# Loading the first modulation weights in 16 pieces, and x and ctx from ScalarE's queue, in a one-core transformer trunk

## The chip, the cores and the metric

The kernel runs on one core of one Trainium2 chip. The metric is the device time of one execution in microseconds (us). Three runs are shown, and one more execution was profiled.

## What is computed

The reference is a trunk of two layers over 256 latent tokens `x` and 256 context tokens `ctx`, each 1024 wide, in float32. The part in front of the first matrix product is this:

```
mod   = silu(c) @ w_mod[l] + b_mod[l]            # 6 x 1024: sh1, sc1, g1, sh2, sc2, g2
mod_c = silu(c_ctx) @ w_mod[l] + b_mod[l]
h  = rmsnorm(x,   norm_mix[l]) * (1 + sc1)  + sh1
hc = rmsnorm(xc,  norm_mix[l]) * (1 + sc1c) + sh1c
z  = h @ w_in[l];  zc = hc @ w_in[l]             # D_IN = 8160 columns, split in 13 parts
...
```

After it come three token mixers (gated linear attention, windowed attention, latent attention), their merge, and a gated feed-forward; layer 1 drops the context stream's output. The first third of `w_mod[0]` (columns 0 to 2047: `sh1`, then `sc1`) and all of `x` and `ctx` are needed before any column of `z` can be computed.

## The kernel before

Everything is kept transposed: 8 tiles of 128 features by 512 tokens (256 of `x`, 256 of `ctx`). A float32 product is made of three float32r products: each operand is split in a high part (a rounding copy on ScalarE) and a low part (a subtraction on VectorE), and TensorE adds high times high (L248), high times low (L249) and low times high (L250). Weights arrive in staging buffers `ws` (three, of 128 x 2048) by loads on SyncE's queue, and are split in blocks of 128 x 1024 into `wh` (ScalarE, L171) and `wl` (VectorE, L172), four buffers each. The tile scheduler puts the instructions of each engine in an order when the program is built; an engine then runs them in that order.

The start of the program (`program`, L1357 to L1375) goes like this:

- `start` (L273) issues the loads of `c`, `c_ctx` and a part of the constants, then the eight quarter-megabyte loads `tok` of `x` and `ctx` (L286), all on SyncE's queue, and `first_units` (L399) issues the first third of `w_mod` in eight loads of 1 MB: three go into the three `ws` buffers, four into the two large buffers that later hold `h` (`hh` and `hl`, here named `wshh` and `wshl`), and the eighth into a `ws` buffer again, once that one has been read. GpSimd's queue loads the biases and gains (`rows`, L296) and the rest of the constants.
- `turn_x` (L356) transposes the tokens on TensorE (L364), copies them out (`x`, L367 and L369) and sums their squares (`acc`, L519 to L523).
- `mod_half(1)` (L416) makes the scales `sc1`: four steps (a `tick` each) of four matmuls over one 1 MB load (L427), then a copy (`modsb`, L432), four transposes (`modt`, L435) and, on VectorE, the sums into `modT` (L440, L441) and the gains (L454). `mod_half(0)` does the same for the shifts `sh1`. `vectors` (L331) transposes `rows`.
- `rstd` (L525) makes the reciprocal root on TensorE (`st`, L531), VectorE (`var`) and GpSimd (`rs`, L537), and `spread` (L540) makes of it a 128 x 512 tile `R` (L556).
- `scaled` (L561) makes `xr` = x times gain times R in 16 instructions on VectorE (L568), and `shifted` (L572) makes of them the high part of h, `hh`, in 16 instructions on ScalarE (L581) and the low part, `hl`, in 16 on VectorE (L582).

The first products are in `gla` (L967): `need` (L183) calls for three blocks of `w_in` (`krgk`, the first query block and the first key block), and `gemms` (L252) makes 144 matmuls of them, 48 each, into the three accumulators `mm`. From them `gkT` (L961, L962), `q` and `k` (L814) are copied out, the gate matmuls `gk` follow (L758, L759), then four groups of value matmuls (L795 to L797, 24 each, `mm` again) and then the first gate product of 512 columns (L248). The `krgk` block comes in three loads of short rows (L155 to L157) behind a GpSimd memset (L152), the others by L137.

Of the kernel before, what the change touches and what calls it, by code (L numbers as in the profile page):

```python
# [7 lines left out]
F32 = mybir.dt.float32  # L8
# [9 lines left out]
P = 128  # L18
D = 1024
KT = 8  # L20
T = 512
# [32 lines left out]
class Trunk:  # L54
# [218 lines left out]
    def start(self):  # L273

        nc, A = self.nc, self.A
# [6 lines left out]
        tok = [[self.tl([P, T], F32, "yh" if b < 2 else "yl", "tok") for _ in range(2)] for b in range(4)]  # L282
        for f in range(2):
            for b in range(4):
                src = A["x" if b < 2 else "ctx"][0, b % 2 * P:(b % 2 + 1) * P, f * T:(f + 1) * T]
                nc.sync.dma_start(out=tok[b][f], in_=src)  # L286
        self.first_units()
        self.prefetch()

# [109 lines left out]
    def first_units(self):  # L399


        nc = self.nc
        ws = lambda: self.tl([P, self.STAGE], F32, "ws", "ws")
        room = [ws() for _ in range(3)]
        for tag in ("hh", "hl"):
            both = self.tl([P, KT * T + 32], F32, tag, "ws" + tag)
            room += [both[:, i * self.STAGE:(i + 1) * self.STAGE] for i in range(2)]
        self.first = {}
        for half in (1, 0):
            for pair in range(4):  # L410
                st = room.pop(0) if room else ws()
                src = self.A["w_mod"][0, pair * 256:(pair + 1) * 256, half * D:(half + 1) * D]
                nc.sync.dma_start(out=st.rearrange("p (k c) -> p k c", k=2), in_=src.rearrange("(k p) c -> p k c", p=P))
                self.first[half, pair] = st

    def mod_half(self, half):  # L416


        nc = self.nc
        ps = self.ps("mod")  # L420
        for pair in range(4):
            w = self.first[half, pair]
            for i in range(2):
                for q in range(2):
                    j = 2 * i + q
                    c0 = i * D + q * 512
                    self.in_order(nc.tensor.matmul(ps[32 * j:32 * j + 32, :], lhsT=self.cs[:, 2 * pair + i, :],  # L427
                                                   rhs=w[:, c0:c0 + 512], start=pair == 0, stop=pair == 3))
            if pair < 3:
                yield  # L430
        sb = self.t([P, 512], name="modsb")
        nc.scalar.activation(out=sb, in_=ps, func=AF.Copy)  # L432
        pt = self.ps("modt")
        for s in range(4):
            self.in_order(nc.tensor.transpose(pt[:, s * P:(s + 1) * P], sb[:, s * P:(s + 1) * P], self.ident))  # L435
        pv = pt.rearrange("p (s i q w) -> p i q s w", s=4, i=2, q=2)
        b0 = half * 8
        m = self.modT[0][:, b0:b0 + 8, :].rearrange("p (q s) w -> p q s w", q=2)
        v = self.vec[0][:, b0:b0 + 8].rearrange("p (q s o) -> p q s o", q=2, o=1).to_broadcast([P, 2, 4, 2])
        nc.vector.tensor_tensor(out=m, in0=pv[:, 0, :, :, 0:2], in1=v, op=ALU.add)  # L440
        nc.vector.tensor_tensor(out=m, in0=pv[:, 1, :, :, 0:2], in1=m, op=ALU.add)  # L441
        if half:
            self.mod_gain(0, 0)
        yield
# [912 lines left out]
    def program(self):  # L1357
        nc = self.nc
        self.bg = None
        tok, rows = self.start()  # L1360
        acc = self.turn_x(tok)
        self.background(self.mod_half(1))
        self.tick(3)
        self.vectors(rows)
        rs = self.rstd(acc, D)
        self.tick(1)
        R = self.spread(rs)
        self.background(self.mod_half(0))
        self.tick(1)
# [2 lines left out]
        for l in range(2):  # L1372
# [35 lines left out]
            q = self.swa_q(l, 0, nq, h)  # L1408
# [111 lines left out]
```

## Time and profile before

| | us |
|---|---|
| median of three runs (lowest, highest) | 1897.33 (1896.89, 1897.68) |
| the profiled execution | 1899.36 |
| its span, first to last instruction | 1897.6 |
| TensorE busy in the span | 1859.0 |
| ScalarE busy in the span | 888.7 |
| VectorE busy in the span | 1231.8 |

The span is what the profile's clock counts from its first instruction; 1.8 us of the profiled execution lie outside it. All times of the trace are us from the start of the span. A row of a timeline has its start, its length, engine, line, operation, tile written and tiles read, shape, count, and in brackets the time for which the engine had been idle and what ended that. "SPq" and "POOLq" are queues that issue loads.

### The profile page before, as it was taken

What the parts mean: (1) busy time and instruction counts of PE and PEld (TensorE: products, weight loads), DVE (VectorE), ACT (ScalarE), POOL (GpSimd) and SP (SyncE); (2) the same over time, 40 slices, a digit from 0 to 9 for tenths busy, and PEclk for the clock granted to TensorE, in tenths of its full rate; (3) what the DMA queues carried; (4) which work ended last, traced back from release to release, by engine and by line L of the source; (5) the groups of instructions that cost most, each with busy time, mean ns of one, the idle gap of its engine ahead of it and who ended that gap; (6) DMA issues with size and microseconds to landing.
All of it is one profiled execution on the core that took longest, in us unless ns stands there. A gap on an engine that the chain in (4) does not pass through costs nothing.

```text
span 1897.6 us, 28869 instructions
## 1 busy us (share of the span) xinstructions
PE 1859.0 (98%) x11482; PEld 1594.6 (84%) x11482; DVE 1231.8 (65%) x2514; ACT 888.7 (47%) x1617; POOL 29.6 (2%) x47
## 2 busy tenths in 40 slices
PE   6999999999999999989999999999999999999998
PEld 4888887788877777888888888899998888899997
DVE  6756454565376655578776755768666678777775
ACT  4654333455454554342223233556455566655554
POOL 2000000000000000000000000000000000000000
PEclk8999999999999999999999999999999999999999
DMA  8533124413134312425555542342443324356553
GB/s 289 145 100 90 56 89 156 137 47 103 53 112 155 99 58 78 138 77 177 178 185 184 182 168 78 106 137 81 123 136 92 112 91 128 99 195 198 172 171 104
DMA packets 217870, 241.01 MB, mean 127 GB/s; under 512 B 18110, under 2 KB 204740, under 8 KB 212616
## 3 DMA queue, kind: packets, MB, share of 16 engines
q1 hardware_dynamic: 216888, 238.13, 39.5%
q8 instruction: 90, 1.47, 0.3%
q0 software_dynamic: 560, 0.52, 0.1%
q10 hardware_dynamic: 288, 0.52, 0.1%
q14 instruction: 44, 0.36, 0.1%
HBM read 234.96 MB, written 4.19 MB: 126 GB/s over the span
## 4 chain that ended last, share of the span: by engine, by line
PE 90%; DVE 4%; ACT 2%; issue 2%; DMA 1%; POOL 1%; SPq 0%; DVEq 0%; POOLq 0%; ACTq 0%
PE mm L248 23%; PE mm L249 23%; PE mm L250 23%; PE S L1138 2%; PE pt L728 2%; PE po L1237 2%; PE po L934 2%; PE po L1151 2%; PE mm L797 2%; PE mm L795 2%; PE mm L796 2%; DVE wl L172 1%; PE S L1218 1%; PE S L1219 1%; ACT wh L171 1%
## 5 line engine op out<-in xcount | busy, mean ns | idle before, releaser
L171 ACT ACTIVATE wh<-ws 128x1024 fp32r<-128x1024 f32 (+3 forms) x352 | 361.9, 1032 | 595.8 <-PE mm L249 449.3
L172 DVE TENSOR_TENSOR wl<-ws,wh 128x1024 fp32r<-128x1024 f32 (+3 forms) x352 | 416.9, 1188 | 296.8 <-ACT wh L171 258.0
L248 PE MATMUL mm<-hh,wh 128*128 128x512 f32 (+1 forms) x1312 | 462.9, 354 | 8.3 <-ACT hh L607 4.5
L249 PE MATMUL mm<-hl,wh 128*128 128x512 f32 (+1 forms) x1312 | 460.2, 351 | 1.0 <-DVE hl L582 0.9
L250 PE MATMUL mm<-hh,wl 128*128 128x512 f32 (+1 forms) x1312 | 460.1, 351 | 0.0
L248 PEld LDWEIGHTS mm<-hh,wh 128*128 128x128 f32 x1312 | 247.5, 189 | 45.5 <-ACT hh L607 5.4
L249 PEld LDWEIGHTS mm<-hl,wh 128*128 128x128 f32 x1312 | 247.8, 189 | 35.0 <-DVE hl L582 1.1
L250 PEld LDWEIGHTS mm<-hh,wl 128*128 128x128 f32 x1312 | 248.2, 189 | 31.9
L248 PE MATMUL mm<-yh,wh 128*128 128x512 f32 (+1 forms) x384 | 130.9, 341 | 0.0
L250 PE MATMUL mm<-yh,wl 128*128 128x512 f32 (+1 forms) x384 | 129.3, 337 | 0.0
L249 PE MATMUL mm<-yl,wh 128*128 128x512 f32 (+1 forms) x384 | 129.2, 336 | 0.0
L249 PE MATMUL mm<-sl,wh 128*128 128x256 f32 (+1 forms) x373 | 122.1, 327 | 0.0
L250 PE MATMUL mm<-sh,wl 128*128 128x256 f32 (+1 forms) x373 | 122.0, 327 | 0.0
L248 PE MATMUL mm<-sh,wh 128*128 128x256 f32 (+1 forms) x373 | 120.7, 325 | 0.0
L709 ACT ACTIVATE p<-S,stat 128x512 f32<-128x512 f32 (+1 forms) x144 | 87.2, 614 | 30.5 <-DVE stat L700 22.8
L248 PE MATMUL mm<-xh,wh 128*128 128x258 f32 x352 | 100.2, 285 | 0.1
L250 PE MATMUL mm<-xh,wl 128*128 128x258 f32 x352 | 99.9, 284 | 0.0
L249 PE MATMUL mm<-xl,wh 128*128 128x258 f32 x352 | 99.9, 284 | 0.0
L698 DVE TENSOR_REDUCE stat<-S 128x1 f32<-128x512 f32 (+1 forms) x144 | 81.5, 595 | 22.0 <-PE S L1138 14.0
L473 DVE SCALAR_TENSOR_TENSOR macc<-ws,cs,macc 128x512 f32<-128x512 f32 x112 | 77.9, 745 | 19.1 <-DMA ws<-in_w_mod 19.0
L248 PEld LDWEIGHTS mm<-yh,wh 128*128 128x128 f32 x384 | 72.6, 189 | 13.1 <-issue 3.3
L1267 DVE SCALAR_TENSOR_TENSOR x<-mm,modT,x 128x256 f32<-128x256 f32 x96 | 44.0, 481 | 60.5 <-PE mm L250 60.3
(311 smaller groups left out, 3463.2 us busy)
## 6 DMA issues: line engine op xcount, KB each, us to landing
ws<-in_w_in SPq DMA_DIRECT2D x54, 1024.0 KB, 5.9
ws<-in_w_mod SPq DMA_DIRECT2D x44, 1024.0 KB, 6.0
ws<-in_w_ffn_in SPq DMA_DIRECT2D x40, 1024.0 KB, 5.1
ws<-in_w_ffn_out SPq DMA_DIRECT2D x16, 896.0 KB, 4.8
ws<-in_w_in SPq DMA_DIRECT2D x18, 512.0 KB, 4.5
ws<-in_w_pa SPq DMA_DIRECT2D x8, 1024.0 KB, 5.2
ws<-in_w_pc SPq DMA_DIRECT2D x8, 1024.0 KB, 6.2
ws<-in_w_pb SPq DMA_DIRECT2D x8, 1024.0 KB, 5.2
```

The source lines that it names most:

```text
L171: self.nc.scalar.activation(out=hv, in_=src, func=AF.Copy)
L172: self.nc.vector.tensor_tensor(out=lv, in0=src, in1=hv.bitcast(F32), op=ALU.subtract)
L248: mm(ps, lhsT=a, rhs=rh[:, n0:n1], start=first and k == 0, stop=False)
L249: mm(ps, lhsT=a, rhs=rl[:, n0:n1], start=False, stop=False)
L250: mm(ps, lhsT=b, rhs=rh[:, n0:n1], start=False, stop=last and k == kt - 1)
L473: nc.vector.scalar_tensor_tensor(out=a, in0=b, scalar=c, in1=a, op0=ALU.mult, op1=ALU.add)
L698: nc.vector.reduce_max(out=mx[:, i:i + 1], in_=s, axis=AX.X)
L709: nc.scalar.activation(out=p, in_=s, func=AF.Exp, scale=scale, bias=nb[:, i:i + 1], accum_out=sm[:, i:i + 1])
L728: nc.tensor.transpose(ps[:, j * 256 + b * P:j * 256 + (b + 1) * P], p[b][:, c:c + P], self.ident)
L795: nc.tensor.matmul(ps[:, :256], lhsT=a, rhs=hi[:, kk, :], start=k8 == 0, stop=False)
L796: nc.tensor.matmul(ps[:, :256], lhsT=a, rhs=lo[:, kk, :], start=False, stop=False)
L1267: self.nc.vector.scalar_tensor_tensor(out=self.X[j][:, c], in0=ps[:, c], scalar=self.modT[l][:, b0 + j, w:w + 1], in1=self.X[j][:, c], op0 ...
```

## The change

It does four things. The eight loads of `x` and `ctx` are issued by ScalarE. The first third of `w_mod` comes in 16 loads of half a megabyte (128 rows of 1024 columns, 4 KB a row) in place of eight of 1 MB with two such row blocks each; eight go into the four `wh` and four `wl` buffers (named `wwh` and `wwl` there), and eight into the two buffers of `h` (`whh`, `whl`), so that the three `ws` buffers are free for `w_in` from the start. `mod_half` reads the pieces. And the ticks are moved: `rstd` follows two steps of `mod_half(1)` in place of three, and `vectors` comes after it.

```diff
@@ start @@
-                nc.sync.dma_start(out=tok[b][f], in_=src)
+                nc.scalar.dma_start(out=tok[b][f], in_=src)
@@ first_units @@
-        ws = lambda: self.tl([P, self.STAGE], F32, "ws", "ws")
-        room = [ws() for _ in range(3)]
+        room = [self.tl([P, D], F32, tag, "w" + tag) for tag in ("wh", "wl") * 4]
         for tag in ("hh", "hl"):
-            both = self.tl([P, KT * T + 32], F32, tag, "ws" + tag)
-            room += [both[:, i * self.STAGE:(i + 1) * self.STAGE] for i in range(2)]
-        self.first = {}
-        for half in (1, 0):
-            for pair in range(4):
-                st = room.pop(0) if room else ws()
-                src = self.A["w_mod"][0, pair * 256:(pair + 1) * 256, half * D:(half + 1) * D]
-                nc.sync.dma_start(out=st.rearrange("p (k c) -> p k c", k=2), in_=src.rearrange("(k p) c -> p k c", p=P))
-                self.first[half, pair] = st
+            four = self.tl([P, KT * T + 32], F32, tag, "w" + tag)
+            room += [four[:, i * D:(i + 1) * D] for i in range(4)]
+        self.first = room
+        for i, st in enumerate(room):
+            k, c0 = i % 8, (1 - i // 8) * D
+            nc.sync.dma_start(out=st, in_=self.A["w_mod"][0, k * P:(k + 1) * P, c0:c0 + D])
@@ mod_half @@
-            w = self.first[half, pair]
             for i in range(2):
+                w = self.first[(1 - half) * 8 + 2 * pair + i]
                 for q in range(2):
                     j = 2 * i + q
-                    c0 = i * D + q * 512
                     self.in_order(nc.tensor.matmul(ps[32 * j:32 * j + 32, :], lhsT=self.cs[:, 2 * pair + i, :],
-                                                   rhs=w[:, c0:c0 + 512], start=pair == 0, stop=pair == 3))
+                                                   rhs=w[:, q * 512:(q + 1) * 512], start=pair == 0, stop=pair == 3))
@@ program @@
-        self.tick(3)
-        self.vectors(rows)
+        self.tick(2)
+        rs = self.rstd(acc, D)
+        self.vectors(rows)
-        rs = self.rstd(acc, D)
-        self.tick(1)
+        self.tick(2)
```

The scheduler makes another order of this, on three places. A row below is an instruction (line, operation, tile written and tiles read, elements of a partition row written), in brackets the completion counters that it waits for: an engine's, or one of eight for loads (DMAHW); xN is a count of equal rows. Lines after the change are lower by 5.

On ScalarE, between the second `modsb` copy and the split of the gate weights `wgkh`, before:

```order
L432 ACTIVATE modsb<-mod 128x512 [waits PE_49]
L171 ACTIVATE wh<-ws 128x1024 [waits DMAHW4_49,DMAHW5_49,DMAHW3_49,Pool_49]
L581 ACTIVATE hh<-xr,modT_68 128x256 [waits DMAHW7_49,DMAHW6_49,DVE_49]
L581 ACTIVATE hh<-xr,modT_68 128x256 x15
L171 ACTIVATE wh<-ws 128x1024 [waits DMAHW6_49]
L265 ACTIVATE wgkh<-wgk 128x512 [waits DMAHW3_49,DMAHW2_49,DMAHW4_49,DMAHW1_49,DMAHW5_49,DMAHW0_49,Pool_49]
```

and with the change:

```order
L427 ACTIVATE modsb<-mod 128x512 [waits PE_49]
L576 ACTIVATE hh<-xr,modT_68 128x256 [waits DMAHW5_49,DMAHW4_49,DMAHW6_49,DMAHW3_49,DVE_49]
L576 ACTIVATE hh<-xr,modT_68 128x256 x15
L171 ACTIVATE wh<-ws 128x1024 [waits DMAHW4_49,DMAHW5_49,DMAHW3_49,Pool_49]
L171 ACTIVATE wh<-ws 128x1024 [waits DMAHW6_49]
L171 ACTIVATE wh<-ws 128x1024 [waits DMAHW7_49]
L265 ACTIVATE wgkh<-wgk 128x512 [waits DMAHW3_49,DMAHW2_49,DMAHW4_49,DMAHW1_49,DMAHW5_49,DMAHW0_49,Pool_49]
```

The first split of `w_in` (the `krgk` block) stood ahead of the 16 `hh` instructions and now stands behind them; VectorE's order moves in the same way, its first `wl` from ahead of the 16 `hl` to behind them.

On TensorE, the first products (`mm_427` is the krgk block's accumulator before; `mm_439`, `mm_440` and `mm_441` are those of krgk, query and key with the change, each with its own `wh` and `wl`), before:

```order
L248 MATMUL mm_427<-hh_345,wh_399 128x256 [waits Activation_49]
L249 MATMUL mm_427<-hl_346,wh_399 128x256 [waits DVE_49]
L250 MATMUL mm_427<-hh_345,wl_400 128x256
L248 MATMUL mm_427<-hh_345,wh_399 128x256 [waits Activation_49]
L249 MATMUL mm_427<-hl_346,wh_399 128x256 [waits DVE_49]
L250 MATMUL mm_427<-hh_345,wl_400 128x256
```

and with the change, behind the first four (high times high and high times low of krgk and of the query block), the next twelve:

```order
L250 MATMUL mm_439<-hh_357,wl_412 128x256 [waits DVE_49]
L248 MATMUL mm_439<-hh_357,wh_411 128x256
L249 MATMUL mm_439<-hl_358,wh_411 128x256
L248 MATMUL mm_441<-hh_357,wh_419 128x256 [waits Activation_49]
L249 MATMUL mm_441<-hl_358,wh_419 128x256
L250 MATMUL mm_440<-hh_357,wl_416 128x256 [waits DVE_49]
L250 MATMUL mm_439<-hh_357,wl_412 128x256
L248 MATMUL mm_440<-hh_357,wh_415 128x256
L249 MATMUL mm_440<-hl_358,wh_415 128x256
L250 MATMUL mm_440<-hh_357,wl_416 128x256
L248 MATMUL mm_439<-hh_357,wh_411 128x256
L250 MATMUL mm_441<-hh_357,wl_420 128x256 [waits DVE_49]
```

Before, the 48 matmuls of krgk come first, each group of three behind the `hh` and `hl` that it reads; now the three blocks take turns, and the 15 matmuls ahead of the last row shown wait for one split after the other; that row waits for the third `wl`, and the 129 from it on for nothing more.

On ScalarE further on, with the change, between the splits for the value products (`wh_425`, `wh_429`) and the copies out of the three accumulators:

```order
L171 ACTIVATE wh_425<-ws_423 128x1024 [waits DMAHW6_49]
L171 ACTIVATE wh_429<-ws_423 128x1024 [waits DVE_49,PE_49]
L956 ACTIVATE gkT_586<-mm_439 16x512 [waits PE_49,Pool_49]
L809 ACTIVATE q_599<-mm_440 128x512 [waits PE_49]
L809 ACTIVATE k_601<-mm_441 128x512 [waits PE_49]
```

`wh_429` takes the buffer of `wh_411`, so its wait on TensorE is for the last matmul of krgk that reads it; the same split stood before ahead of the krgk copies with no wait on TensorE, since krgk was done early. The first value matmul waits for the copy `q_599`, whose accumulator it takes. Past the value products each engine's instructions stand in the same order as before.

## Rows read from the trace of the kernel before

**Rows 1.** The page's part 1: busy us, share of the span, instructions.

```profile
PE 1859.0 (98%) x11482; PEld 1594.6 (84%) x11482; DVE 1231.8 (65%) x2514; ACT 888.7 (47%) x1617; POOL 29.6 (2%) x47
```

**Rows 2.** Windows of 50 us: window, length, busy us of PE, PEld, DVE, ACT, POOL, clock, DMA.

```profile
0.00:50.00 50.00, 34.04 (x195) 22.30 (x196) 31.04 (x77) 22.95 (x44) 11.75 (x26) 0.83 0.85 283
50.00:100.00 50.00, 50.00 (x361) 44.34 (x360) 34.41 (x72) 28.35 (x47) 0.00 (x0) 1.00 0.44 129
...
300.00:350.00 50.00, 50.00 (x243) 34.60 (x242) 20.12 (x37) 11.38 (x21) 1.01 (x1) 1.00 0.55 188
```

**Rows 3.** Timeline, start: ScalarE's first instruction, and loads issued on SyncE's queue.

```profile
0.74 1.28 ACT L322 ACT_TABLE_LOAD   x1 [0.74 <-PEq L1510]
...
1.94 0.90 SPq L286 DMA_DIRECT2D tok<-in_x  x2
...
6.33 3.46 SPq L413 DMA_DIRECT2D ws<-in_w_mod  x3
...
16.82 1.34 SPq L413 DMA_DIRECT2D ws<-in_w_mod  x1
```

**Rows 4.** Windows, columns as in rows 2; the last two are DMA share and GB/s.

```profile
4.00:9.00 5.00, 2.22 (x9) 1.75 (x9) 0.53 (x3) 0.22 (x1) 3.08 (x7) 1.00 0.95 306
...
18.00:31.00 13.00, 10.04 (x44) 4.15 (x48) 5.31 (x17) 1.88 (x5) 2.45 (x4) 0.56 1.02 420
```

**Rows 5.** Timeline of TensorE, 14 to 40 us.

```profile
21.22 1.93 PE L427 MATMUL mod<-ws,cs 128*32 128x512 f32 x8 [1.42 <-DMA ws<-in_w_mod]
23.08 0.69 PE L337 MATMUL ps<-cst,rows 128*128 128x128 f32 x2
23.56 1.71 PE L531 MATMUL st<-ones,acc 128*128 128x1 f32 x8
25.20 1.93 PE L427 MATMUL mod<-wshh,cs 128*32 128x512 f32 x8
...
34.38 1.03 PE L427 MATMUL mod<-ws,cs 128*32 128x512 f32 x8
...
37.99 0.39 PE L248 MATMUL mm<-hh,wh 128*128 128x256 f32 x1 [1.19 <-ACT hh L581]
39.31 0.39 PE L249 MATMUL mm<-hl,wh 128*128 128x256 f32 x1 [0.94 <-DVE hl L582]
```

**Rows 6.** Timeline of VectorE, 10 to 60 us.

```profile
16.17 3.07 DVE L523 TENSOR_TENSOR acc<-acc,sq 128x512 f32<-128x512 f32 x4
...
30.42 6.35 DVE L568 SCALAR_TENSOR_TENSOR xr<-x,gain,R 128x256 f32<-128x256 f32 x16 [0.76 <-PE R L556]
...
37.04 0.17 DVE L441 TENSOR_TENSOR modT<-modt,modT 128x16 f32<-128x16 f32 x1
37.63 1.23 DVE L172 TENSOR_TENSOR wl<-ws,wh 128x1024 fp32r<-128x1024 f32 x1 [0.42 <-ACT wh L171]
...
49.25 2.36 DVE L172 TENSOR_TENSOR wl<-ws,wh 128x1024 fp32r<-128x1024 f32 x2
```

**Rows 7.** Timeline of ScalarE, 36 to 60 us.

```profile
36.48 1.06 ACT L171 ACTIVATE wh<-ws 128x1024 fp32r<-128x1024 f32 x1 [0.39 <-DMA ws<-in_w_in]
...
37.44 6.48 ACT L581 ACTIVATE hh<-xr,modT 128x256 fp32r<-128x256 f32 x16
...
47.06 0.59 ACT L961 ACTIVATE gkT<-mm 16x512 fp32r<-16x512 f32 x1 [0.72 <-PE mm L250]
...
58.73 0.60 ACT L814 ACTIVATE q<-mm 128x512 f32<-128x512 f32 x1
```

**Rows 8.** Windows, columns as in rows 2: TensorE's clock in the first products.

```profile
40.10:43.50 3.40, 3.40 (x18) 3.40 (x18) 3.40 (x9) 3.40 (x10) 0.00 (x0) 0.50 0.96 280
43.50:58.00 14.50, 14.50 (x125) 14.37 (x124) 10.27 (x20) 6.64 (x11) 0.00 (x0) 1.00 0.64 187
```

**Rows 9.** Timeline of TensorE: the gate matmuls and the first matmul of 512 columns.

```profile
57.96 0.50 PE L758 MATMUL gk<-gkT,wgkh 64*128 64x512 f32 x2
...
69.63 0.39 PE L248 MATMUL mm<-hh,wh 128*128 128x512 f32 x1
```

## The prediction

> **What bounds the kernel now.** I read the page's busy times first: TensorE is busy for 1859.0 of 1897.6 us [rows 1]. The windows of 50 us then say where the rest is: 34.04 us busy in the first 50, and from 50 us on 50.00 of 50 in each of the six windows to 350 [rows 2]. So the start is a chain of waits, and what stands behind it is a wall of matmuls. A microsecond gained or lost before the wall goes through to the end, all the more as every engine's order past the value products is the same after the change. I therefore measure the change at one point, the first matmul of 512 columns, at 69.63 us [rows 9].
>
> The chain up to it, in the timelines: VectorE ends the sums of squares at 16.17 + 3.07 = 19.24 [rows 6]; TensorE takes the third megabyte of w_mod at 21.22, after a wait for its load, then transposes the gains, makes `st`, and takes the fourth megabyte from 25.20 to 27.13 [rows 5]. From there `modsb`, `modt`, `R` lead to `xr` at 30.42, `modT` ends at 37.21 [rows 6], `hh` starts at 37.44 [rows 7]. **H** is that start in what follows. TensorE's second product runs at 39.31 [rows 5], 1.87 us after H, because krgk's split had been done ahead of `hh` (36.48 [rows 7]) and of `hl` (37.63 [rows 6]). From then on it works without a gap: 144 matmuls to 57.96, 11.67 us of gate and value matmuls to 69.63 [rows 9].
>
> **Term 1, H comes earlier: 37.44 to 35.6, -1.8 us.** ScalarE's first instruction starts at 0.74, while the first `tok` load is issued at 1.94 [rows 3]; with the loads on ScalarE's queue they start up to 1.2 us sooner. From 18 to 31 us the DMA engines' share is 1.02 at 420 GB/s [rows 4], so all that the queues can win is that earlier start: w_mod lands some 1.2 us earlier. At 420 GB/s a megabyte (1.05 million bytes) takes 2.5 us; the third was there at 21.22, so the fourth was there at 23.7, and will be at 22.5. It waited for TensorE then, and that is what the moved ticks mend. With the change `st` follows two steps and the sum (19.24): 1.71 us to 21.0, the gains' transposes 0.69 (lengths of [rows 5], overlapping a little) to 21.6, two steps at 1.93 to 25.5, against 27.13. All behind it keeps its lengths, so `modT` ends at 37.21 - 1.6 = 35.6, and `hh` follows at once, since no split occupies ScalarE. The second half does not hold it: the last piece should land near 32.4 (the last step began at 34.38 before [rows 5]; eighth megabyte by 21.22 + 5 x 2.5 = 33.7, less 1.2). Lower end: TensorE at full clock there (a step is 1.03 in the last of [rows 5] and 1.93 in the others), and then the landing at 32.4 is the limit, with half a step and 1.8 us from the last step's end to `modT`: 34.7, or -2.7. Upper end: `tok` shares the engines with w_mod, arrives 2.5 us later and moves the sum of squares by as much: 38.1, or +0.7.
>
> The eight issues on ScalarE cost nothing: its first work on tokens waits for the transposes of all of the first four. The eighth load of w_mod, which waited for a buffer until 16.82 [rows 3], no longer waits; with the engines' share at 1 that moves no byte.
>
> **Term 2, the products start later after H: 20.5 to 27.8 us, +7.3.** Before, 57.96 - 37.44 = 20.5 us lie between H and the end of the 144 matmuls. With the new order ScalarE first makes all 16 `hh`, at 6.48 [rows 7], and only then the first `wh`, 1.06: H + 7.5. VectorE's 16 `hl` run a step behind `hh` and end before that. Then the three `wl`, 1.18 each (two in 2.36 [rows 6]), end at H + 11.1, and TensorE's order puts only 15 matmuls ahead of the third. The other 129 take 0.116 each at full clock (125 in 14.50 [rows 8]): 15.0. To this I add what a low clock costs. Before, TensorE idled for most of 35.4 to 39.3; the granted clock fell to 0.50, the lower level of 1.2 GHz, at 40.10 and was back at 43.50 [rows 8]: half of 3.4 us is 1.7. Now the engine idles for about 9 us ahead of the products, and I take the same 1.7. Sum: 11.1 + 15.0 + 1.7 = 27.8. Ends: the low clock costs nothing (it falls and recovers in the idle time), or lasts twice as long: 26.1 to 29.5.
>
> That the weights would have to wait for data is unlikely: the three loads of krgk and the two blocks behind them no longer wait for a buffer and follow w_mod directly.
>
> **Term 3, a new stall behind the products: +1.4.** `wh_429` now waits for krgk's last matmul, six from the end, and stands on ScalarE ahead of the copies of krgk and of the query. TensorE works 6 x 0.116 = 0.7 us more and then waits for the query's copy: the split of 1.06, `gkT`'s 0.59 and q's 0.60, each starting 0.1 before the end of the one ahead (as 37.44 after 36.48 + 1.06 shows) [rows 7], end some 2.1 us after krgk's last matmul. 2.1 - 0.7 = 1.4; lower end 0. The gate matmuls move into the value products, and I count no stall there: by the same sum their operands are ready 0.3 us before they are reached.
>
> **Sum.** -1.8 + 7.3 + 1.4 = +6.9 us at the reference point: 76.5 in place of 69.6. The profiled execution took 1899.36 us, of which 1897.6 are the span, and would take 1906.3; the median of the runs is 2.03 us below it, at 1897.33, so I predict **1904.2 us**. All low ends together give +2.9, all high ends +11.1.
>
> **Rivals.**
>
> *The loads win much more (the other side: not slower).* If two queues moved the bytes faster than one, H would come earlier still. The point from which it decides: H must come 6.9 us before 35.6, at 28.7, for no change. The second half must have landed 2.3 us before that (half a step and 1.8 us), at 26.4. Some 11 MB (8.4 of w_mod, 2.1 of tokens, 0.5 of constants) from 2 us on would then need 450 GB/s throughout; the rows show 306 on token loads and 420 on w_mod's [rows 4]. At 480 GB/s it lands at 24.9, and H is 27.2, if `xr` keeps up: 1895.8, and each us that they landed earlier still would take one more off. TensorE's 1.93 us steps and `xr`'s 6.35 us speak against it too. By the rows I leave it 4%, half of that for faster by over 0.2%. The Trainium skill, page "DMA: Bandwidth & Descriptors", section "Issuing engines are not separate DMA queues", says that DMAs started by several engines run on the same 16 DMA engines, and that a second issuing engine saves only the time to issue. By that rule this rival has no chance at all; the share of 1.02 on one queue agrees, but no row of before has two such queues at work.
>
> *The gain and the loss nearly cancel.* H at 34.7, no cost of the clock, no stall for q: +2.9, 1900.2, within 0.2% (3.8 us), which is about what a measurement of this kernel can tell from no change. For it speaks that each low end is possible by itself; against it, that Term 2's 11.1 us come from an order that is fixed. 8%.
>
> *The smaller loads are slower.* Pieces of half a megabyte may move worse than those of one. The quarter-megabyte token loads ran at 306 GB/s [rows 4], though with rows half as long; w_mod's 8.4 MB at that rate take 27.4 us, not 20.0, which puts the last piece at 39.8, H at 42.1, and the time at 1904.2 + 6.5 = 1910.7. Against it: the packets keep their 4 KB rows, and up to eight loads are in flight. 6%. The Trainium skill, same page, "Measured (HBM→SBUF, 128 partitions, SWDGE, issued from GpSimd)", tells one to batch DMAs to at least 1 MiB; its 341 GB/s for that size stands below the 420 that this trace shows for a queue of them, so it describes single transfers, and no run here shows half of it.
>
> *The clock stays low longer.* From 18 to 31 us TensorE's mean clock was 0.56 [rows 4] with many short waits. If the new stop-and-go start kept it at the low level through the 15.0 us of products, that would cost another 6 us at most: 1907 to 1910. 6%.
>
> **How the numbers follow.** The forecast has 76%; with the slower loads and the slow clock, slower by over 0.2% has 88%, no change 10% (the cancelling case and half of the first rival), faster 2%. The range runs from 1901.0, near the boundary of no change, to 1908.5, the high ends short of all of them together; it leaves out the fast case, most of the cancelling one and the two dear ones' upper parts, together under 2 in 10.
>
> **What the profile will show.** Right: `hh` starts near 35.6 and the first `wh` of w_in some 6.5 us behind it; TensorE's matmuls of 256 columns run densely only from near 47, then 15 us and the low clock; one idle stretch of about 1.4 us at line 790, ended by the query's copy; the first matmul of 512 columns near 76.5; windows from 100 us on as before. Wrong: `hh` before 33, a dense start before 43, or the lag at the reference point not found again at the end.

## The result, and the profile after

| | us |
|---|---|
| changed kernel, median of seven runs (lowest, highest) | 1912.95 (1908.23, 1915.88) |
| kernel before, seven runs, the three of the first table among them | 1897.37 (1896.89, 1903.94) |
| ratio, 95% interval | 1.0059 (1.0043 to 1.0075) |
| forecast (range) | 1904.2 (1901.0 to 1908.5) |
| profiled execution, and its span | 1915.54, 1913.8 |

The change makes the kernel slower, as forecast, but by about 11 us (0.59% of 1897.37; 8 to 14 by the interval) in place of 6.9, and the median lies above the range. The two medians lie further apart, by 15.6; since the kernel before took 1901.4 to 1902.5 in the later measurements, I go by the ratio.

The page and the windows of 50 us, to be read against [rows 1, 2]:

```profile
PE 1862.8 (97%) x11482; PEld 1594.8 (83%) x11482; DVE 1232.2 (64%) x2514; ACT 889.6 (46%) x1617; POOL 29.7 (2%) x47
```

```profile
0.00:50.00 50.00, 23.18 (x121) 11.60 (x122) 26.47 (x73) 19.12 (x39) 11.83 (x26) 0.89 0.75 254
50.00:100.00 50.00, 48.72 (x320) 43.72 (x320) 32.24 (x64) 28.00 (x45) 0.00 (x0) 0.98 0.53 158
...
300.00:350.00 50.00, 50.00 (x240) 36.38 (x239) 24.82 (x47) 15.55 (x28) 2.02 (x2) 1.00 0.48 161
```

Nearly all of the loss up to the reference point is in the first 50 us: TensorE is busy for 10.9 us less there and for 1.3 us less in the next 50. From 100 us on it is full, as before.

**The tokens.** TensorE's timeline at the token transposes (start, length; the idle time and what ended it in brackets), then VectorE's:

```profile
16.48 0.48 PE L364 MATMUL ps<-cst,tok 128*128 128x128 f32 x1 [1.44 <-DMA tok<-in_ctx]
20.38 3.03 PE L364 MATMUL ps<-cst,tok 128*128 128x128 f32 x13 [3.43 <-DMA tok<-in_ctx]
...
27.18 1.05 PE L526 MATMUL st<-ones,acc 128*128 128x1 f32 x8 [1.08 <-DVE acc L518]
```

```profile
24.06 3.07 DVE L518 TENSOR_TENSOR acc<-acc,sq 128x512 f32<-128x512 f32 x4
...
34.48 6.36 DVE L563 SCALAR_TENSOR_TENSOR xr<-x,gain,R 128x256 f32<-128x256 f32 x16 [0.34 <-PE R L551]
40.75 0.17 DVE L435 TENSOR_TENSOR modT<-modt,vec 128x16 f32<-128x16 f32 x1
40.95 0.17 DVE L436 TENSOR_TENSOR modT<-modt,modT 128x16 f32<-128x16 f32 x1
...
48.63 3.50 DVE L172 TENSOR_TENSOR wl<-ws,wh 128x1024 fp32r<-128x1024 f32 x3
```

TensorE's wait for the last token ends at 20.38, and the sum of squares ends at 24.06 + 3.07 = 27.13; before, it ended at 19.24 [rows 6]. `st`, which needs the sum, starts at 27.18 in place of 23.56 [rows 5], and since it stands ahead of two steps of `mod_half(1)` in TensorE's order, these, `R`, `xr` and `modT` are late too. The last token load was also issued late (ScalarE's queue, then ScalarE itself):

```profile
6.12 4.11 ACTq L286 DMA_DIRECT2D tok<-in_ctx  x2
10.27 1.28 ACT L322 ACT_TABLE_LOAD   x1 [10.27 <-DMA wwh<-in_w_mod]
```

The first of the eight is issued at 0.74, the last only at 9.90, and ScalarE's first work behind it, at 0.74 before [rows 3], waits until 10.27 for a landing of w_mod. What the DMA engines moved from 2 to 16 us, by queue (packets, MB, share of the engines; q1 is SyncE's, q10 ScalarE's, q0 GpSimd's), before and after:

```profile
q1 hardware_dynamic: 1822, 4.18, 82.8%
q0 software_dynamic: 528, 0.51, 13.1%
```

```profile
q1 hardware_dynamic: 802, 2.41, 45.5%
q10 hardware_dynamic: 1113, 2.03, 40.2%
q0 software_dynamic: 495, 0.50, 13.0%
```

Before, one queue moved the 2.1 MB of tokens and, behind them, 2.1 MB of weights. Now the two queues share the engines about evenly, in sum hardly faster (4.95 MB in these 14 us for 4.70). A ctx load of 256 KB then takes 9.9 us from its issue to its landing (the table of DMA issues, first 30 us):

```profile
tok<-in_x ACTq DMA_DIRECT2D x4, 256.0 KB, 2.9
tok<-in_ctx ACTq DMA_DIRECT2D x4, 256.0 KB, 9.9
```

The Trainium skill, "DMA: Bandwidth & Descriptors", section "Queues, rings and completion order", says that a DMA engine takes turns between the queues that have work, packet by packet; the nearly even 2.03 and 2.41 MB agree, though no single turns are seen here.

**The splits, the products and what follows**, on ScalarE and TensorE, to be read against [rows 5, 7, 9]:

```profile
41.16 6.50 ACT L576 ACTIVATE hh<-xr,modT 128x256 fp32r<-128x256 f32 x16 [2.49 <-DVE modT L436]
47.56 2.94 ACT L171 ACTIVATE wh<-ws 128x1024 fp32r<-128x1024 f32 x3
...
67.04 1.06 ACT L171 ACTIVATE wh<-ws 128x1024 fp32r<-128x1024 f32 x1 [10.13 <-PE mm L249]
68.01 0.57 ACT L956 ACTIVATE gkT<-mm 16x512 fp32r<-16x512 f32 x1
68.48 0.57 ACT L809 ACTIVATE q<-mm 128x512 f32<-128x512 f32 x1
```

```profile
48.66 0.58 PE L248 MATMUL mm<-hh,wh 128*128 128x256 f32 x1 [9.27 <-ACT wh L171]
...
67.55 0.28 PE L250 MATMUL mm<-hh,wl 128*128 128x256 f32 x1
69.11 0.39 PE L790 MATMUL mm<-wh,hh 128*128 128x256 f32 x1 [1.28 <-ACT q L809]
...
70.23 0.49 PE L753 MATMUL gk<-gkT,wgkh 64*128 64x512 f32 x1
70.57 0.39 PE L754 MATMUL gk<-gkT,wgkl 64*128 64x512 f32 x1
...
82.16 0.40 PE L248 MATMUL mm<-hh,wh 128*128 128x512 f32 x1
```

H, the start of `hh`, is at 41.16 (forecast 35.6). The first `wh` follows 6.4 us behind it, the last of the 144 matmuls starts at 67.55, 26.39 behind H; the value products wait until the query's copy, and the first matmul of 512 columns is at 82.16 in place of 69.63: +12.53 (forecast +6.9). The clock in the products (windows; the clock is the third number from the end):

```profile
50.20:51.50 1.30, 1.30 (x8) 1.30 (x8) 1.30 (x2) 0.82 (x2) 0.00 (x0) 0.50 0.29 59
52.20:67.80 15.60, 15.60 (x132) 15.42 (x131) 1.76 (x2) 1.82 (x2) 0.00 (x0) 0.99 0.51 158
```

At the end of the span the lag is 1913.8 - 1897.6 = 16.2, so 3.7 us are added behind the reference point, with no idle time that would show them. The last experiment is about these.

### The profile page after: what moved, and what is told of

Its sections match the earlier page's. It is cut to its first block, busy times and chain, and to the rows that moved or that the text cites. A ratio compares the mean times of both kernels' runs of the same rounds, so it can differ in the third digit from the quotient of the medians.

```text
span 1913.8 us, 28873 instructions
## 1 busy us (share of the span) xinstructions
PE 1862.8 (97%) x11482; PEld 1594.8 (83%) x11482; DVE 1232.2 (64%) x2514; ACT 889.6 (46%) x1617; POOL 29.7 (2%) x47
## 4 chain that ended last, share of the span: by engine, by line
PE 90%; DVE 4%; ACT 2%; DMA 2%; issue 1%; POOL 0%; SPq 0%; DVEq 0%; POOLq 0%; ACTq 0%
PE mm L248 23%; PE mm L249 23%; PE mm L250 22%; PE S L1133 2%; PE pt L723 2%; PE po L1232 2%; PE po L929 2%; PE po L1146 2%; PE mm L792 2%; PE mm L790 2%; PE mm L791 2%; DVE wl L172 1%; PE S L1213 1%; ACT wh L171 1%; PE S L1214 1%
## 5 line engine op out<-in xcount | busy, mean ns | idle before, releaser
L248 PEld LDWEIGHTS mm<-yh,wh 128*128 128x128 f32 x384 | 72.5, 189 | 13.2 <-issue 3.3
```

The source lines that it names most:

```text
L248: mm(ps, lhsT=a, rhs=rh[:, n0:n1], start=first and k == 0, stop=False)
```

## The experiments

The points of each profile, in us: end of the sums of squares, H, the last of the 144 matmuls counted from H, from there to the first matmul of 512 columns, and where this stands; then the time ratio to the kernel before in the same measurement. The kernel before took 1901.4 to 1902.5 in the measurements of the experiments, so ratios are compared, not times; the expectations' times were counted from 1897. "after_a", "after_b" and "before_a" are the two kernels unaltered.

| kernel | sum | H | last of 144 | to 512 | at | ratio (95%) |
|---|---|---|---|---|---|---|
| before | 19.24 | 37.44 | +20.31 | +11.88 | 69.63 | |
| changed | 27.13 | 41.16 | +26.39 | +14.61 | 82.16 | 1.0059 (1.0043 to 1.0075) |
| tok_sync | 18.72 | 37.22 | +26.40 | +14.61 | 78.23 | 1.0050 (1.0033 to 1.0067) |
| tok_only | 28.68 | 41.95 | +20.50 | +11.88 | 74.33 | 1.0011 (1.0000 to 1.0022) |
| pieces_only | 18.01 | 36.72 | +26.43 | +14.60 | 77.75 | 1.0055 (1.0040 to 1.0070) |
| split_first | 26.72 | 40.71 | +21.43 | +11.88 | 74.02 | 1.0013 (1.0003 to 1.0022) |
| sync_split_first | 18.10 | 37.80 | +20.24 | +11.88 | 69.92 | 0.9983 (0.9973 to 0.9994) |
| two_queues | 21.32 | 39.47 | +20.23 | +11.88 | 71.58 | 1.0006 (0.9995 to 1.0016) |
| six_split_first | 21.19 | 38.68 | +20.48 | +11.88 | 71.04 | 1.0004 (0.9991 to 1.0017) |
| tok_six | 21.70 | 36.62 | +27.57 | +14.69 | 78.88 | one run |
| copies_first | 26.57 | 40.38 | +26.60 | +13.89 | 80.87 | one run |
| after_a | 26.69 | 39.02 | +27.59 | +16.21 | 82.82 | 1.0050 (1.0036 to 1.0065) |
| after_b | 26.96 | 40.66 | +26.70 | +14.61 | 81.97 | one run |
| before_a | 18.38 | 37.51 | +20.26 | +11.88 | 69.65 | one run |

**tok_sync: the token loads back on SyncE's queue.**

```diff
-                nc.scalar.dma_start(out=tok[b][f], in_=src)
+                nc.sync.dma_start(out=tok[b][f], in_=src)
```

> The changed kernel with one word undone: x and ctx load from SyncE's queue again, ahead of the 16 pieces. Theory (the tokens came late because they share the DMA engines with the pieces): the sum of squares ends near 19 us instead of 27.1, hh starts at 35 to 37 instead of 41.2, the rest keeps its lengths (26.5 us from there to the end of the 144 products, a stall of 1.4), the first matmul of 512 columns is at 76 to 78 and the time is 1903 to 1907. Rival 1 (pieces of half a megabyte move worse than whole ones): the sum of squares ends near 19, but the pieces land late and hh still starts at 39 to 41; 1908 or more. Rival 2 (the moved ticks are to blame): hh at 38 or later as well, with the pieces landed by 33.

The sum ends at 18.72 and H is 37.22, 3.9 us earlier than in the changed kernel; all behind H is as there. H and the reference point (78.23) lie 0.2 us above what was expected, and neither rival came out. The queue of the tokens is what made H late. But H does not come to 35.6. TensorE waits for the weights now:

```profile
33.05 1.05 PE L422 MATMUL mod<-whl,cs 128*32 128x512 f32 x4 [1.33 <-DMA whl<-in_w_mod]
34.35 1.05 PE L422 MATMUL mod<-whl,cs 128*32 128x512 f32 x4 [0.25 <-DMA whl<-in_w_mod]
36.11 0.66 PE L430 MATMUL modt<-cst,modsb 128*128 128x128 f32 x4 [0.70 <-ACT modsb L427]
```

The last piece lands at 34.35, when the last step of the kernel before began too (34.38 [rows 5]). With all the tokens ahead of it, the stream of loads sets H, and the moved ticks win nothing. Its time came out at 1911.04 (beside 1901.6 for the kernel before), above the 1903 to 1907 expected, which had been counted from 1897.

**tok_only: only the token loads moved, in the kernel before.**

```diff
-                nc.sync.dma_start(out=tok[b][f], in_=src)
+                nc.scalar.dma_start(out=tok[b][f], in_=src)
```

> The kernel before with one word changed: x and ctx from ScalarE's queue, w_mod in eight loads of 1 MB as before, the order of the splits as before. Theory: the tokens now share the engines with w_mod's first loads, the sum of squares ends at 22 to 27 us instead of 19.2 and hh starts 2 to 6 us later than 37.4; the 144 products still end 20.5 us behind it; 1899.5 to 1903.5. Rival (it is the size of the pieces): hh at 36 to 37.5, no change, 1896 to 1897.5.

The same fault without a single small piece: the sum ends at 28.68, later than the 22 to 27 expected, H is 41.95, 4.5 us late, and 4.7 us are left at the reference point. The ratio shows less, 0.11% or 2 us, with an interval from 0 to 4 us. So it is not the size of the pieces.

**pieces_only: only the 16 pieces, in the kernel before's buffers.**

```diff
-                nc.sync.dma_start(out=st.rearrange("p (k c) -> p k c", k=2), in_=src.rearrange("(k p) c -> p k c", p=P))
+                for i in range(2):
+                    nc.sync.dma_start(out=st[:, i * D:(i + 1) * D], in_=src[i * P:(i + 1) * P])
```

> The kernel before with each 1 MB load of w_mod cut into two of half a megabyte into the same buffers; tokens on SyncE's queue, ticks as before. The scheduler answers by putting the 16 hh ahead of the first split, as in the changed kernel. Theory: hh starts near where it was (36.5 to 38.5), the 144 products end 26 to 27 us behind it (20.5 before), the stall of 1.4 and the slower value products appear: 1904 to 1907. Rival (smaller loads are slower): hh at 40 or later, 1908 or more. Rival (the order costs nothing): 1897 to 1898.

ScalarE's timeline:

```profile
36.72 6.49 ACT L582 ACTIVATE hh<-xr,modT 128x256 fp32r<-128x256 f32 x16 [1.17 <-DVE modT L442]
43.12 2.93 ACT L171 ACTIVATE wh<-ws 128x1024 fp32r<-128x1024 f32 x3
```

H is 36.72, 0.7 us earlier than before: halves are not slower than whole megabytes. Yet the products end 26.43 behind H, as in the changed kernel, and the kernel is 0.55% slower. Cutting the loads alone makes the scheduler put the splits behind `hh`; neither the other buffers nor the ticks are needed for it.

**split_first: the split of krgk ahead of `hh` and `hl`, in the changed kernel.**

```diff
             if l == 0:
+                if not self.dry:
+                    self.split_block(0)
                 h = self.shifted(xr)
@@ shifted @@
-                nc.scalar.activation(out=hi[:, c], in_=tt[:, c], func=AF.Identity, bias=b)
+                self.in_order(nc.scalar.activation(out=hi[:, c], in_=tt[:, c], func=AF.Identity, bias=b))
```

(and the same for `hl` on VectorE).

> The changed kernel with the split of the gate weights (krgk) put ahead of the 16 hh and 16 hl by hand, which gives back the old order of the products. Theory: hh still starts at 41 to 42, but the 144 products end 20 to 21 us behind it, the stall at the value products is gone and these take 11.7 us again: the first matmul of 512 columns at 73 to 74.5 and 1900 to 1903. Rival (the weights come late, or a low clock holds the products up, not the order): still 25 us or more behind hh, 1907 or more.

ScalarE's timeline, and TensorE's:

```profile
38.12 1.05 ACT L171 ACTIVATE wh<-ws 128x1024 fp32r<-128x1024 f32 x1
40.71 6.50 ACT L576 ACTIVATE hh<-xr,modT 128x256 fp32r<-128x256 f32 x16 [1.54 <-DVE modT L436]
```

```profile
62.35 0.50 PE L753 MATMUL gk<-gkT,wgkh 64*128 64x512 f32 x2
62.69 0.40 PE L754 MATMUL gk<-gkT,wgkl 64*128 64x512 f32 x2
```

One split of 1.05 us, put into a time in which ScalarE waited for `modT` anyway, takes 5.0 us off the way from H to the last of the 144, and the stall and the slow value products are gone with it: from H to the reference point it is 33.3 us in place of 41.0. The ratio falls to 1.0013. The 21.43 lies 0.4 us above the expected 20 to 21; the granted clock was 0.50 from 42 to 47 us. The order is the larger of the two faults.

**sync_split_first: both undone.** The edits of tok_sync and split_first together.

> Both suspects undone in the changed kernel: x and ctx on SyncE's queue ahead of the pieces, and the krgk split ahead of hh and hl by hand. Theory (these two are the whole loss): hh starts at 37 to 37.8, the 144 products end 20.5 to 21.6 us behind it, no stall at the value products, the first matmul of 512 columns at 69.3 to 71: the time of the kernel before to 0.1%, though the 16 pieces and the moved ticks are still there. Rival (something else of the change costs as well): the first matmul of 512 columns at 72 or later, slower by over 0.1%. Rival (freed of its two faults the change gains): 68 or earlier.

69.92 against 69.63: the two faults are the whole loss up to the reference point, and the rest of the change neither wins nor costs up to there. The two add up: the order costs 8.1 us at the reference point (82.16 to 74.02) or 8.3 (78.23 to 69.92), the queue 3.9 (82.16 to 78.23) or 4.1 (74.02 to 69.92). The runs are 0.17% faster than the kernel before (1899.22 for 1901.36), more than the 0.1% expected and with an interval that leaves out no change. This profile does not explain it, since nothing came earlier, and the cause stays open; how much the pace behind the reference point differs is shown below. I don't count it as a gain.

**two_queues and six_split_first: arrangements in which both queues carry tokens**, with the krgk split ahead.

```diff
-                nc.scalar.dma_start(out=tok[b][f], in_=src)
+                (nc.scalar if f == 0 else nc.sync).dma_start(out=tok[b][f], in_=src)
```

> As sync_split_first, but the four loads of the tokens' first half are on ScalarE's queue and the four of the second half on SyncE's, all ahead of the pieces in time. Theory (what hurts is sharing the engines with w_mod, not the queue): the sum of squares ends at 17 to 19 us, hh starts at 36 to 37.3, the first matmul of 512 columns at 68 to 69.8; 0 to 1.5 us under the kernel before. Rival (loads on ScalarE's queue are slow whatever stands beside them): sum of squares after 22, hh at 40 or later, slower than before by 3 us or more.

```diff
-                nc.scalar.dma_start(out=tok[b][f], in_=src)
+                (nc.sync if f and b > 1 else nc.scalar).dma_start(out=tok[b][f], in_=src)
```

> The two best arrangements together: six token loads on ScalarE's queue and the last two on SyncE's as in tok_six, the krgk split ahead of hh as in split_first. Theory (before hh the stream of loads is the limit, so no order of these loads wins more than a us): hh at 36.7 to 37.6, 144 products 20.5 to 21.5 us behind, first matmul of 512 columns at 69 to 70.5: the time of before within 0.15%. Rival (the queues do help once the two faults are gone): first matmul of 512 columns at 68 or earlier and 0.1% to 0.2% faster than before.

Both miss their expectation, by some 2 us and 1 us: H is 39.47 and 38.68, the sum of squares ends at 21.3 and 21.2. Neither is faster than the kernel before. In two_queues the rival's H of 40 was not reached either. All its token loads were issued by 4.13, ahead of the first piece (4.51), and yet the sum ended 2.6 to 3.2 us later than in tok_sync and sync_split_first; why was not found. The sum no longer held anything up there (`st` starts at 21.37 without a wait), but the last piece of w_mod was there at 35.88, 1.5 us later than in tok_sync and sync_split_first (34.35), and the krgk block came late as well. In six_split_first H is 2.1 us later than in tok_six with the same loads: the wait for the last piece ended at 34.95 in place of 33.75, and the granted clock fell to 0.50 in the last step, which ended at 36.87. So the landing of the same loads differed by 1.2 us between these two profiles, and the lower clock goes with the rest.

**tok_six: the last two token loads on SyncE's queue, in the changed kernel.** The edit is the second one just shown, without the split.

> The changed kernel with only the last two token loads (ctx, second half) back on SyncE's queue ahead of the pieces; six stay on ScalarE's. It parts the two ways in which the tokens were late: if it was the issue of the last one, held until 9.90 us by the load counter that it shares with a piece, the sum of squares now ends at 18.5 to 20.5 us and hh starts at 37 to 38; if it is that the token loads share the engines with the pieces, the six on ScalarE's queue are still late, the sum ends at 21 to 26 and hh starts at 38.5 to 41.

The scheduler left one piece ahead of the two loads on SyncE's queue. The sum ends at 21.70, 5.4 us earlier than in the changed kernel but 2.5 later than before, so the six loads on ScalarE's queue are still late, as sharing says. H, at 36.62, is below both expectations, because a sum at 21.70 no longer holds H up: the last piece does, at 33.76. The held issue is not needed for the harm, though: in tok_only all token loads were issued by 7.10, and the last one still landed when TensorE's wait ended at 20.38. What remains is how much the hold until 9.90 adds in the changed kernel; this was not tried by itself. ScalarE's queue and the start of its first instruction in tok_only:

```profile
5.67 1.39 ACTq L286 DMA_DIRECT2D tok<-in_ctx  x2
7.10 1.28 ACT L322 ACT_TABLE_LOAD   x1 [7.10 <-DMA cst<-in_consts]
```

**copies_first: the split that waits for krgk behind the copies.** Three edits, of which the last is shown: the first products call for one block less ahead, and the second value block's split is called for after the three copies, and pinned behind them:

```diff
         self.gla_qk(prj, "k", todo[2][0], T, 1.0)
+        if l == 0 and not self.dry:
+            self.split_block(4)
```

> The changed kernel with the split for the second value block (wh_429, which waits for krgk's last matmul) put behind the copies of krgk, query and key on ScalarE. Theory (it is the split that holds the copies up): the stall at the first value matmul falls from 1.3 us to 0.2 to 0.6, hh and the products stay where they are, and the first matmul of 512 columns is 0.7 to 1.2 us earlier against hh (41.0 behind it in the changed kernel). Rival (the copies are late by themselves): the stall stays at 1.2 to 1.4.

```profile
67.76 0.39 PE L792 MATMUL mm<-wh,hh 128*128 128x256 f32 x1 [0.51 <-ACT q L811]
```

The stall falls from 1.28 to 0.51, and the reference point comes from 41.00 behind H to 40.49: 0.5 us, less than the 0.7 to 1.2 expected, since the products before it took 0.2 more this time. The split was the cause of most of the stall.

**after_a, after_b, before_a: the two kernels unaltered, for the part behind the reference point.**

> The changed kernel once more, unaltered. Its first profile lost 12.5 us up to the first matmul of 512 columns and 3.7 us more behind it, where a matmul of 512 columns takes 233.3 ns for long stretches in place of 228.9, at the same granted clock. Theory (the pace of those stretches differs from execution to execution, whatever the kernel): first matmul of 512 columns at 81.5 to 82.8 again, but the lag to the end anywhere from 10 to 17 us, and runs that differ by several us. Rival (the later start puts this kernel into the slow pace): the stretch from 1000 to 1200 us again at 232.7 in both repeats.

> The same kernel a third time, for its profile alone: under the theory its pace from 1000 to 1200 us need not be that of the other two; under the rival it is 232.7 again.

> The kernel before, unaltered, for a second profile. Theory: first matmul of 512 columns at 69.3 to 70 again; pace from 1000 to 1200 us between 228.8 and 232.7, and not bound to be the 229.5 of its first profile. Rival (the pace belongs to the kernel): 229.5 again.

Windows from 1020 to 1180 us, in which TensorE does little but matmuls of 512 columns; the number behind TensorE's busy time is its matmuls. The changed kernel first, then after_b, before and before_a:

```profile
1020.00:1180.00 160.00, 160.00 (x689) 129.84 (x688) 98.34 (x141) 43.53 (x56) 0.00 (x0) 1.00 0.50 165
```

```profile
1020.00:1180.00 160.00, 160.00 (x701) 131.31 (x700) 101.22 (x148) 44.94 (x59) 0.09 (x1) 1.00 0.49 165
```

```profile
1020.00:1180.00 160.00, 160.00 (x698) 131.06 (x697) 102.45 (x154) 44.80 (x59) 0.53 (x1) 1.00 0.48 156
```

```profile
1020.00:1180.00 160.00, 160.00 (x690) 129.90 (x689) 101.79 (x153) 44.54 (x58) 0.53 (x1) 1.00 0.47 154
```

At the same granted clock of 1.00 and with no gap, one execution gets through 701 matmuls and another through 689, and each kernel shows both paces. Over all fourteen profiles this window has 689 or 690 matmuls in seven and 698 to 701 in the other seven, kernels with the old and with the new order among both; from the reference point to the end it is 1829.2 to 1832.1 us in the first seven and 1825.2 to 1829.1 in the others. So the pace belongs to the execution, as far as these profiles go. It decides several us: after_b passes the reference point 12.3 us behind the kernel before and ends only 1909.4 - 1897.6 = 11.8 behind it; the first profile had 12.5 and 16.2. The expectation of 81.5 to 82.8 for the reference point was kept by after_b and missed by 0.02 in after_a, where the clock fell once more behind the stall:

```profile
70.00:74.00 4.00, 4.00 (x19) 3.85 (x19) 3.87 (x8) 2.52 (x5) 0.00 (x0) 0.58 0.77 247
```

The same repeat shows that H is no constant of the kernel: it is 39.02 there and 41.16 in the first profile, though the sums end within 0.5 us of each other. The two steps behind `st` run from 28.44 to 32.05 in the first profile and from 28.00 to 29.92 in after_a, at these granted clocks (the first profile above):

```profile
26.00:31.00 5.00, 3.92 (x27) 1.70 (x26) 3.05 (x9) 0.00 (x0) 1.99 (x3) 0.75 1.03 420
26.00:31.00 5.00, 3.68 (x33) 1.87 (x30) 3.15 (x10) 1.01 (x3) 1.99 (x3) 1.00 1.02 416
```

What after_a wins there it loses behind H, where the clock is low in more of the products and again behind the stall. What decides the clock in either place was not found.

## Why the forecast was wrong in size

**Term 1 is the step that failed.** "H comes earlier: 37.44 to 35.6, -1.8 us" was +3.7 in the first profile, an error of 5.5, the whole of what the sum lacked at the reference point (12.5 for 6.9), with smaller errors that cancel beside it. In after_a, where the steps behind `st` ran at full clock, H was +1.6 and the error 3.4; in after_b it was 5.1. Two sentences of it were wrong. The first is "with the loads on ScalarE's queue they start up to 1.2 us sooner": the first was issued 1.2 us sooner, but the last only at 9.90, and they landed later, since the loads of the other queue are not behind them but beside them. "The eight issues on ScalarE cost nothing" left out that an issue can wait for a landing; what that adds was not tried by itself. The upper end named the sharing, and priced it at 2.5 us of the sum, the time that it gives one megabyte. In fact SyncE's queue moved 2.41 MB beside the tokens' 2.03, and the sum was 7.9 us late. That H moved by no more than 3.7 is because `st` had slack: before, it stood behind the third megabyte and ran at 23.56 [rows 5], now at 27.18, 3.6 us later. The second is that "w_mod lands some 1.2 us earlier": in the changed kernel the last four pieces were issued from 21.2 to 24.2 and landed 9.1 to 9.9 us after their issue, the last one thus between 33.3 and 34.1, and with the tokens first (tok_sync) it was there at 34.35, not at 32.4. So the gain on which the term stood did not exist either: with all tokens ahead of the pieces H is 37.22 (tok_sync), 36.72 (pieces_only) and 37.80 (sync_split_first), from 0.7 us under the kernel before to 0.4 over it.

The rule that the prediction set against the first rival (the Trainium skill, "DMA: Bandwidth & Descriptors", section "Issuing engines are not separate DMA queues") was right, for no kernel with token loads on both queues was faster than the one before. But it was only half used: it also says that the DMAs of several engines interleave. Here that meant that the urgent loads lost their place, and that half was not carried into Term 1.

**Term 2 was right in mechanism and a little too large.** 20.5 to 27.8 us forecast; by the same points it was 26.5. `wh` stood 6.4 us behind H (forecast 6.5), the third `wl` ended at 48.63 + 3.50 = 52.13, 10.97 behind H (11.1). The difference is the low clock: 1.7 us had been added for it, and the clock was back at full speed from about 52.2, when the dense part began, so that 67.67 - 52.13 - 15.0 = 0.5 is left for it. In after_a and tok_six the same sum leaves 1.7 (66.73 - 49.98 - 15.0 and 64.31 - 47.61 - 15.0), as forecast, so the 1.7 holds for some executions. Before, though, the low clock had cost nothing: before_a has none in its products and the same 20.3 us (last section). split_first shows that the order is the cause, and pieces_only that 16 loads are enough for it.

**Term 3 was right.** 1.4 us forecast, and 69.11 - 67.55 less one matmul's 0.12 is 1.44, ended by the query's copy; copies_first shows the split to be its cause.

**A term was missing.** "The gate matmuls move into the value products, and I count no stall there": there is none, but they cost more. From the stall to the reference point it is 13.05 us for 11.67 [rows 9], 1.4 more. Before, the forward and the backward gate matmul ran together, on 64 rows each ("x2" in [rows 9] and in split_first's rows above: two of L753 from 62.35, two of L754 from 62.69), some 0.7 us for all four. With the change the two of each direction stand alone, the backward ones 17 matmuls behind the forward ones: 70.57 - 70.23 = 0.34 for one, so 1.4 for the four. That is about half of the 1.4; the rest lies in the 96 value matmuls and was not parted further. The kernels with the old order have 11.88 us from the last of the 144 on; this part belongs to the order too.

**The sum.** +3.7 + 6.0 + 1.4 + 1.4 = 12.5. In after_a the shares differ and the sum hardly does: +1.6 + 7.2 + 1.4 + 3.0 = 13.2. The expected sign that "the lag at the reference point [is] not found again at the end" came true as well, by 3.7 us in the first profile; the repeats show that this is the pace, not the change, and that it falls out in either direction. The two measurements of the whole change (1.0059 and 1.0050) put it at 11.2 and 9.5 us.

**The rivals.** Faster loads: no, 4.95 MB moved for 4.70. Smaller loads slower: no, by pieces_only. A clock that stays low: no in the first profile; in after_a it took 1.2 us more in the products and, falling again from 70 us on, 1.6 behind them (16.21 for 14.61). The 6 us that the prediction puts on it are the price of 15 us at the low level (7.5, less the 1.7 in the sum); all 129 matmuls at it would have cost 15.0 us, 13.3 more than the 1.7 in the sum. The cancelling case needed Term 1's gain.

## What to carry to other kernels

A load that others wait for should stand ahead of the bulk loads on the same queue; here, on a second queue, the first of them was issued 1.2 us earlier and all of them shared the engines with the bulk loads, and the sum that needs them came 7.9 us later. Before a bulk load is cut into more pieces, see what the scheduler makes of it: 16 loads for 8 put one split of 1 us behind 16 other instructions, and that cost 7.7 us on a path without slack. And a bound such as "it arrives 2.5 us later" should be worked out from how much the other queue has to move at the same time, not from one load of it.

## What was not expected of the hardware

- TensorE has two paces at one granted clock. In long stretches matmuls of 512 columns start every 0.228 us in one execution and every 0.232 in another (160 us for 701 or for 689 matmuls, clock 1.00 in both). Each kernel shows both; what decides was not found. In the changed kernel it makes some 4 us from the reference point to the end (1827.3 to 1831.6), and this is larger than several of the effects above.
- The low clock of the first products [rows 8] is no constant of the kernel: the second profile of the kernel before has none there (the same stretch, clock 1.00 and 28 matmuls for 18), and yet its reference point is at 69.65 and not earlier: the faster matmuls wait for the splits instead, 0.50 us of it in one piece for the third. From 38 to 44 us 36 start in place of 27, from 44 to 47 us 19 in place of 28.

```profile
40.10:43.50 3.40, 3.40 (x28) 3.40 (x27) 3.40 (x9) 3.40 (x9) 0.00 (x0) 1.00 0.95 279
```

```profile
46.47 0.38 PE L248 MATMUL mm<-hh,wh 128*128 128x256 f32 x1 [0.50 <-ACT wh L171]
```
